# The last layer norm of a two-layer hybrid decoder: which tiles' statistics ScalarE forms, how epsilon is added, and how VectorE's work is ordered at the end

## The chip, the core and the metric

The kernel runs on one core of a Trainium2 chip. A core has five engines that run their own instruction streams in order and wait for each other on semaphores: TensorE (PE in the profile, its weight loads PEld), VectorE (DVE), ScalarE (ACT), GpSimd (POOL) and SyncE (SP, which here only issues transfers). SBUF is the on-chip memory of 128 partitions, PSUM the banks into which TensorE accumulates. The metric is the device time of one execution, in microseconds.

## The reference

Two post-norm layers over 1024 positions of width 1024. Layer 0 mixes tokens with a gated DeltaNet, layer 1 with an S5 state-space model; each has a memory attention beside its mixer and a squared-ReLU MLP behind it. What the change touches is the second norm of each layer:

```python
def layer_norm(x, g, b):
    xf = x.astype(jnp.float32)
    mu = jnp.mean(xf, axis=-1, keepdims=True)
    var = jnp.mean(jnp.square(xf - mu), axis=-1, keepdims=True)
    return ((xf - mu) * lax.rsqrt(var + LN_EPS) * g.astype(jnp.float32) + b.astype(jnp.float32)).astype(x.dtype)

for i in range(DEPTH):
    ...
    x = layer_norm(DN_ALPHA * x + h, ln1_g[i], ln1_b[i])
    f = jnp.square(jax.nn.relu(x @ mlp_w1[i])) @ mlp_w2[i]
    x = layer_norm(DN_ALPHA * x + f, ln2_g[i], ln2_b[i])
```

## The kernel before

Every product is formed from a high and a low part of each operand, as three matmuls of 128x512 into one PSUM bank (lines 397 to 399). The 1024 positions are eight tiles of 128 rows, tile 0 to tile 7.

The second half of the MLP (`mlp_second`) runs most of its products in a scheme with fewer multiplications and ends in `mlp_last`. There, for each tile and each half c of its 512 columns, TensorE runs a group of twelve matmuls into one of three PSUM banks in turn, VectorE adds the bank to the tile's row sum `y` (line 938), and after the second half `done` calls `layer_norm` for the tile. The text below writes 6a and 6b for the halves of tile 6.

`layer_norm` has two ways to its statistics. Without `junk`, VectorE runs one BN_STATS for each half (line 509), BN_AGGR (510) for mean and variance, and forms 1024 times (variance plus epsilon) (511). With `junk`, ScalarE sums each half (502), VectorE makes the negative mean (503), ScalarE sums the squares about it (505), and VectorE adds the two sums and epsilon (506). ScalarE must write its elementwise results somewhere; `junk` is a PSUM bank that nobody reads. GpSimd raises the result to the power -0.5 (512). VectorE then does two passes over the tile, called the centre (522: subtract the mean, times gamma) and the scale (523: times the power, plus beta). In the very last tile of the last layer the centre is line 514, and the scale runs in two halves (517), each stored at once (518). The factor 1024 leaves the power smaller by 32, so gamma is multiplied by 32 on ScalarE after it is loaded (2346 for the second norm, 2307 for the first).

In layer 0 the normalised tile goes through TensorE transposes (530) into the operands of layer 1, ScalarE and VectorE splitting them into high and low parts (534, 535). In layer 1 it is stored.

The order of instructions on every engine is not that of the code. `settle` takes all instructions of the program, their dependencies and a price for each, gives every instruction a due time from TensorE's sequence, and simulates the engines: on each, the open instruction that is due first goes next. The resulting order is fixed with dependencies. In that simulation an instruction may start when its predecessors' full length and a lag are over; a matmul behind a matmul needs only its busy time.

Constants lie at the start of SBUF in one pool, each in slots of 32 bytes; the pools of working tiles follow. In the built program before, the working tiles begin at byte 18,432 of a partition, and every one of the 3,288 tiles of 1 KB and more starts on a multiple of 512 bytes.

Of the kernel before, what the change touches and what calls it, by code (L numbers as in the profile page):

```python
# [10 lines left out]
F32 = mybir.dt.float32  # L11
F32R = mybir.dt.float32r
AF = mybir.ActivationFunctionType
ALU = mybir.AluOpType
AX = mybir.AxisListType

P = 128
# [16 lines left out]
class Trunk:  # L34
    def __init__(self, ctx, tc, a):
        self.tc = tc
        self.nc = nc = tc.nc
        self.a = a
        self.uid = 0
        self.turn = 0  # L40
        self.proj = 0
        self.soon = set()
        self.home, self.fixed = {}, set()
        self.cp = ctx.enter_context(tc.tile_pool(name="cp", bufs=1))
        self.sp = ctx.enter_context(tc.tile_pool(name="sp", bufs=1))
        self.ps = ctx.enter_context(tc.tile_pool(name="ps", bufs=1, space=bass.MemoryType.PSUM))
        self.dp = ctx.enter_context(tc.tile_pool(name="dp", bufs=1, space=bass.MemoryType.DRAM))
        self.ident = self.const("ident", [P, P])
        make_identity(nc, self.ident)
        self.const("pad", [P, 112])  # L50
        self.eps_ln = self.const("eps_ln", [P, 1])
        nc.gpsimd.memset(self.eps_ln, 1024 * 1e-5)
        self.mhalf = self.const("mhalf", [P, 4])
        nc.gpsimd.memset(self.mhalf, -0.5)
        self.half = self.const("half", [P, 4])
        nc.gpsimd.memset(self.half, 0.5)
# [5 lines left out]
    def settle(self, first, last, reach=0.0, ahead=15.0, passes=1, margin=0.0, late=0.0, hold=1e3):  # L62
# [118 lines left out]
        for _ in range(passes):  # L181
# [36 lines left out]
            while len(order) < n:  # L218
                first_ = None
                drift = free[E.PE] - due[turns[head]] if head < len(turns) else 0.0  # L220
                for e in names:
                    pick = None
                    for x in open_[e]:
                        if e == E.PE and x != turns[head] and due[x] > due[turns[head]] + reach - 1e-6:
                            continue
                        s = room(x) if fresh[x] else 0.0
                        if s is None:
                            continue
                        if e == E.SP:
                            s += 1  # L230
                        r = max(ready[x], s, free[e], due[x] - ahead if e != E.PE else 0.0)
                        if cost[x][2] > 1.5:
                            r = max(r, due[x] + drift - hold)
                        if e == E.PE and kind == "fr" and ins[x].ins[0].dtype == F32:
                            r += 0.15
                        other = 1.28 if sets[x] not in (None, table) else 0.0
                        k = (0, due[x] + other, r, x) if r <= free[e] + 0.1 else (1, r + other, due[x], x)
                        if pick is None or k < pick[0]:
                            pick = k, r, x
                    if pick and (first_ is None or pick[1:] < first_[1:]):  # L240
                        first_ = pick
                assert first_, f"no order: {len(order)} of {n}"
                r, x = first_[1:]
                e = ins[x].engine
                busy, length, moves = cost[x]
                if sets[x] not in (None, table):
                    table, busy, length = sets[x], busy + 1.28, length + 1.28
                if moves:
                    served = max(served, r + length - moves) + moves
                    length = served - r + late  # L250
                if port[x]:
                    r = max(r, locked)
                    locked = r + busy
                if e == E.PE:
                    lost += r - free[e]
                    kind = (kind + "fr"[ins[x].ins[0].dtype == F32R])[-2:]
                    gone.add(x)
                    while head < len(turns) and turns[head] in gone:
                        head += 1
                open_[e].remove(x)  # L260
                free[e] = r + busy
                order.append(x)
                for nm in fresh[x]:
                    t = self.home[nm][:2]
                    slots[t].remove(min(slots[t]))
                    turn[t].remove(nm)
                for y in after[x] + then[x]:
                    same = e == E.PE and ins[y].engine == e
                    ready[y] = max(ready[y], r + (0.0 if x not in deps[y] else busy if same else length + lag + (margin if ins[y].engine == E.PE else 0.0)))
                    wait[y] -= 1  # L270
                    if not wait[y]:
                        open_[ins[y].engine].append(y)
                for nm in uses(ins[x]):
                    if nm in users:
                        over[nm] = max(over[nm], r + length + (3 if ins[x].opcode == 'DMACopy' and e == E.Pool and self.home[nm][1] == 'gb' else 0.0))
                        todo[nm] -= 1
                        if not todo[nm] and nm not in behind and self.home[nm][:2] in slots:
                            slots[self.home[nm][:2]].append(over[nm] + lag)
# [214 lines left out]
    def layer_norm(self, y, gb, junk=None, last=None):  # L493

        nc = self.nc
        st = self.tile("st", [P, 2, 6], F32, "bn")
        halves = y if isinstance(y, list) else [y[:, c * HALF:(c + 1) * HALF] for c in range(2)]
        mv = self.tile("st", [P, 4], F32, "mv")
        if junk is not None:
            s = st.rearrange("p a b -> p (a b)")  # L500
            for c in range(2):
                nc.scalar.activation(junk, halves[c], AF.Copy, accum_out=s[:, c:c + 1])
            nc.vector.tensor_scalar(mv[:, 0:1], s[:, 0:1], s[:, 1:2], -1.0 / 1024, op0=ALU.add, op1=ALU.mult)
            for c in range(2):
                nc.scalar.activation(junk, halves[c], AF.Square, bias=mv[:, 0:1], accum_out=s[:, 4 + c:5 + c])
            nc.vector.scalar_tensor_tensor(mv[:, 2:3], s[:, 4:5], s[:, 5:6], self.eps_ln, op0=ALU.add, op1=ALU.add)
        else:
            for c in range(2):
                nc.vector.bn_stats(st[:, c, :], halves[c])
            nc.vector.bn_aggr(mv[:, 0:2], st)  # L510
            nc.vector.tensor_scalar(mv[:, 2:3], mv[:, 1:2], 1024.0, 1024 * 1e-5, op0=ALU.mult, op1=ALU.add)  # L511
        nc.gpsimd.tensor_tensor(mv[:, 3:4], mv[:, 2:3], self.mhalf[:, 0:1], op=ALU.pow)  # L512
        if last is not None:
            nc.vector.scalar_tensor_tensor(y, y, mv[:, 0:1], gb[0], op0=ALU.subtract, op1=ALU.mult)
            for c in range(2):
                c = slice(c * HALF, (c + 1) * HALF)
                nc.vector.scalar_tensor_tensor(y[:, c], y[:, c], mv[:, 3:4], gb[1][:, c], op0=ALU.mult, op1=ALU.add)
                nc.sync.dma_start(last[:, c], y[:, c])
            return
        parts = [(y, slice(0, 1024))] if not isinstance(y, list) else [(y[c], slice(c * HALF, (c + 1) * HALF)) for c in range(2)]  # L520
        for o, c in parts:
            nc.vector.scalar_tensor_tensor(o, o, mv[:, 0:1], gb[0][:, c], op0=ALU.subtract if junk is None else ALU.add, op1=ALU.mult)
            nc.vector.scalar_tensor_tensor(o, o, mv[:, 3:4], gb[1][:, c], op0=ALU.mult, op1=ALU.add)
# [1816 lines left out]
    def mlp_block(self, i, B, ahead, xd, side, out, more):  # L2340
        new = []

        def done(y, tau):
            if tau == 0:
                self.gb2 = self.load_gb(self.a["ln2_g"][i:i + 1], self.a["ln2_b"][i:i + 1])
                self.nc.scalar.activation(self.gb2[0], self.gb2[0], AF.Copy, scale=32.0)
                if more:
                    new.extend(self.new_xT())
            self.layer_norm(y[tau], self.gb2, self.psum("mm", "jk") if tau in ((), (5, 6))[i] else None, last=out[tau] if tau == 7 and not more else None)
            if tau < 7 or more:  # L2350
                self.nc.sync.dma_start(out[tau], y[tau])
            if more and tau == 7:
                self.last_x(y, new, more(new))
            elif more and tau < 6:
                self.transpose_x(y[tau], tau, new)
# [91 lines left out]
```

## Time and profile before

| | us |
|---|---|
| runs, median of 3 | 2513.36 |
| lowest and highest run | 2511.43, 2513.53 |
| the profiled execution | 2512.02 |
| its span in the profile | 2510.3 |
| TensorE busy | 2471.1 (98%) |
| VectorE busy | 1969.6 (78%) |
| ScalarE busy | 1283.0 (51%) |
| GpSimd busy | 435.9 (17%) |

The span is what the trace covers; the profiled execution's own time is 1.7 us longer. In the trace's timelines a row has the start, the duration, the engine, the line, the operation, the tiles written and read, and in brackets how long the engine idled before it and what ended that. A line is that of the kernel before.

### The profile page before, as it was taken

What the parts mean: (1) busy time and instruction counts of PE and PEld (TensorE: products, weight loads), DVE (VectorE), ACT (ScalarE), POOL (GpSimd) and SP (SyncE); (2) the same over time, 40 slices, a digit from 0 to 9 for tenths busy, and PEclk for the clock granted to TensorE, in tenths of its full rate; (3) what the DMA queues carried; (4) which work ended last, traced back from release to release, by engine and by line L of the source; (5) the groups of instructions that cost most, each with busy time, mean ns of one, the idle gap of its engine ahead of it and who ended that gap; (6) DMA issues with size and microseconds to landing.
All of it is one profiled execution on the core that took longest, in us unless ns stands there. A gap on an engine that the chain in (4) does not pass through costs nothing.

```text
span 2510.3 us, 36952 instructions
## 1 busy us (share of the span) xinstructions
PE 2471.1 (98%) x12181; PEld 2063.9 (82%) x12181; DVE 1969.6 (78%) x3676; ACT 1283.0 (51%) x2730; POOL 435.9 (17%) x673
## 2 busy tenths in 40 slices
PE   8999999999999999999999999999999999999998
PEld 6888887887887887888888888888887888888886
DVE  7786888777779798879988957786687666578788
ACT  6665555554556576554444244564365555544441
POOL 1232332414002023212210123112011000000000
PEclk9999999999999999999999999999999999999999
DMA  6464585767854567487454489669736434574532
GB/s 211 119 163 125 138 257 135 237 189 226 270 166 157 192 218 236 154 297 240 148 161 134 157 245 301 214 216 331 259 131 206 155 143 164 216 255 133 168 105 97
DMA packets 320769, 481.17 MB, mean 192 GB/s; under 512 B 110225, under 2 KB 141153, under 8 KB 320577
## 3 DMA queue, kind: packets, MB, share of 16 engines
q1 hardware_dynamic: 293056, 423.76, 51.9%
q0 software_dynamic: 25216, 50.86, 6.9%
q10 hardware_dynamic: 2304, 4.20, 0.4%
q8 instruction: 96, 1.57, 0.3%
q14 instruction: 97, 0.79, 0.1%
HBM read 321.91 MB, written 156.73 MB: 191 GB/s over the span
## 4 chain that ended last, share of the span: by engine, by line
PE 87%; DVE 5%; ACT 3%; DMA 2%; issue 2%; POOL 1%; SPq 0%; DVEq 0%; POOLq 0%; ACTq 0%
PE q L398 7%; PE q L397 7%; PE q L399 7%; PE tm L397 4%; PE tm L399 4%; PE tm L398 4%; PE pA L399 3%; PE pA L397 3%; PE pA L398 3%; PE wi L397 3%; PE wi L399 3%; PE wi L398 3%; PE pC L399 2%; PE pC L397 2%; PE pC L398 2%; PE pB L397 2%
## 5 line engine op out<-in xcount | busy, mean ns | idle before, releaser
L397 PE MATMUL q<-wkh,hkh 128*128 128x512 f32 x784 | 306.2, 391 | 0.7 <-ACT G L1886 0.7
L398 PE MATMUL q<-wkl,hkh 128*128 128x512 f32 x784 | 305.9, 390 | 0.5 <-DVE wkl L901 0.5
L399 PE MATMUL q<-wkh,hkl 128*128 128x512 f32 x784 | 305.4, 390 | 0.0
L900 ACT CAST wkh<-wr 128x512 fp32r<-128x512 f32 x168 | 104.9, 624 | 237.5 <-PE q L398 186.2
L512 POOL TENSOR_TENSOR mv<-mv,mhalf 128x1 f32<-128x1 f32 x32 | 26.7, 833 | 858.9 <-DVE mv L511 634.6
L397 PEld LDWEIGHTS q<-wkh,hkh 128*128 128x128 f32 x784 | 147.2, 188 | 32.2 <-ACT G L1886 1.6
L398 PEld LDWEIGHTS q<-wkl,hkh 128*128 128x128 f32 x784 | 147.3, 188 | 31.0 <-DVE wkl L901 1.1
L399 PEld LDWEIGHTS q<-wkh,hkl 128*128 128x128 f32 x784 | 147.2, 188 | 30.5
L901 DVE TENSOR_TENSOR wkl<-wr,wkh 128x512 fp32r<-128x512 f32 x168 | 115.5, 688 | 65.8 <-issue 55.6
L397 PE MATMUL wi<-xTh,wih 128*128 128x512 f32 x384 | 159.9, 416 | 0.2 <-ACT qT L1098 0.2
L398 PE MATMUL wi<-xTl,wih 128*128 128x512 f32 x384 | 152.6, 397 | 0.0
L399 PE MATMUL wi<-xTh,wil 128*128 128x512 f32 x384 | 152.4, 397 | 0.0
L901 DVE TENSOR_TENSOR hkl<-hr,hkh 128x512 fp32r<-128x512 f32 x196 | 133.9, 683 | 0.2 <-ACT hkh L900 0.2
L900 ACT CAST hkh<-hr 128x512 fp32r<-128x512 f32 x196 | 120.8, 616 | 1.3 <-DMA hr<-hd 1.2
L397 PE MATMUL tm<-so 128*128 128x512 f32 x280 | 109.8, 397 | 0.0
L1621 ACT CAST so<-or 128x1024 fp32r<-128x1024 f32 x70 | 72.0, 1049 | 59.5 <-DMA or<-wod 42.0
L1622 DVE TENSOR_TENSOR so<-or,so 128x1024 fp32r<-128x1024 f32 x70 | 84.5, 1220 | 16.1 <-ACT so L1621 16.0
L398 PE MATMUL tm<-so 128*128 128x512 f32 x224 | 88.2, 394 | 0.0
L399 PE MATMUL tm<-so 128*128 128x512 f32 x224 | 87.4, 391 | 0.0
L399 PEld LDWEIGHTS wi<-xTh,wil 128*128 128x128 f32 x384 | 72.7, 189 | 14.8
L397 PEld LDWEIGHTS wi<-xTh,wih 128*128 128x128 f32 x384 | 73.2, 191 | 12.5 <-ACT qT L1098 0.6
L398 PEld LDWEIGHTS wi<-xTl,wih 128*128 128x128 f32 x384 | 73.2, 191 | 11.6 <-issue 0.3
(588 smaller groups left out, 7381.8 us busy)
## 6 DMA issues: line engine op xcount, KB each, us to landing
hr<-hd SPq DMA_DIRECT2D x212, 256.0 KB, 2.8
wr<-in_w_dram SPq DMA_DIRECT2D x56, 512.0 KB, 5.0
hd<-u SPq DMA_DIRECT2D x92, 256.0 KB, 2.0
w1r<-in_w_dram SPq DMA_DIRECT2D x32, 512.0 KB, 3.5
hd<-hid SPq DMA_DIRECT2D x60, 256.0 KB, 2.3
hd<-p SPq DMA_DIRECT2D x60, 256.0 KB, 2.2
w1r<-in_w_dram SPq DMA_DIRECT2D x56, 256.0 KB, 3.6
wir<-in_w_in_dram SPq DMA_DIRECT2D x24, 512.0 KB, 3.9
```

The source lines that it names most:

```text
L397: mm(ps, a[0], b[0], start=start, stop=False, skip_group_check=onto)
L398: mm(ps, a[0], b[1], start=False, stop=False, skip_group_check=onto)
L399: mm(ps, a[1], b[0], start=False, stop=stop, skip_group_check=onto)
L512: nc.gpsimd.tensor_tensor(mv[:, 3:4], mv[:, 2:3], self.mhalf[:, 0:1], op=ALU.pow)
L900: nc.scalar.copy(hi, s)
L901: nc.vector.tensor_tensor(lo, s, f32(hi), op=ALU.subtract)
L1621: nc.scalar.copy(hi, r)
L1622: V.tensor_tensor(lo, r, f32(hi), op=ALU.subtract)
```

## The change

A constant of two columns, (0, epsilon), is added. Without `junk`, BN_AGGR now writes to two spare columns, and one addition of that constant yields mean and variance plus epsilon side by side; the centre reads the mean from there, so it needs the addition. With `junk`, the second norm (whose `y` is one tile, not a list of two) takes two operations for what was one: the scaled sum of squares, then epsilon. The first norm keeps its one operation. The second norm's power is then the true one, and ScalarE no longer multiplies its gamma by 32. In layer 1 ScalarE forms the statistics of tiles 3, 4 and 5 in place of 5 and 6. In `settle`, within the last 60 us of the simulated TensorE time, an instruction may follow its predecessor on the same engine after the busy time and 0.06 us.

```diff
         nc.gpsimd.memset(self.eps_ln, 1024 * 1e-5)
+        self.eps2 = self.const("eps2", [P, 2])
+        nc.gpsimd.memset(self.eps2[:, 0:1], 0.0)
+        nc.gpsimd.memset(self.eps2[:, 1:2], 1e-5)
         self.mhalf = self.const("mhalf", [P, 4])
...
                 for y in after[x] + then[x]:
-                    same = e == E.PE and ins[y].engine == e
-                    ready[y] = max(ready[y], r + (0.0 if x not in deps[y] else busy if same else length + lag + (margin if ins[y].engine == E.PE else 0.0)))
+                    same = ins[y].engine == e and (e == E.PE or not moves and spot[x] > now - 60.0)
+                    ready[y] = max(ready[y], r + (0.0 if x not in deps[y] else busy + (0.0 if e == E.PE else 0.06) if same else length + lag + (margin if ins[y].engine == E.PE else 0.0)))
...
-        mv = self.tile("st", [P, 4], F32, "mv")
+        mv = self.tile("st", [P, 6], F32, "mv")
...
-            nc.vector.scalar_tensor_tensor(mv[:, 2:3], s[:, 4:5], s[:, 5:6], self.eps_ln, op0=ALU.add, op1=ALU.add)
+            if isinstance(y, list):
+                nc.vector.scalar_tensor_tensor(mv[:, 1:2], s[:, 4:5], s[:, 5:6], self.eps_ln, op0=ALU.add, op1=ALU.add)
+            else:
+                nc.vector.tensor_scalar(mv[:, 4:5], s[:, 4:5], s[:, 5:6], 1.0 / 1024, op0=ALU.add, op1=ALU.mult)
+                nc.vector.tensor_tensor(mv[:, 1:2], mv[:, 4:5], self.eps2[:, 1:2], op=ALU.add)
         else:
             for c in range(2):
                 nc.vector.bn_stats(st[:, c, :], halves[c])
-            nc.vector.bn_aggr(mv[:, 0:2], st)
-            nc.vector.tensor_scalar(mv[:, 2:3], mv[:, 1:2], 1024.0, 1024 * 1e-5, op0=ALU.mult, op1=ALU.add)
-        nc.gpsimd.tensor_tensor(mv[:, 3:4], mv[:, 2:3], self.mhalf[:, 0:1], op=ALU.pow)
+            nc.vector.bn_aggr(mv[:, 4:6], st)
+            nc.vector.tensor_tensor(mv[:, 0:2], mv[:, 4:6], self.eps2, op=ALU.add)
+        nc.gpsimd.tensor_tensor(mv[:, 3:4], mv[:, 1:2], self.mhalf[:, 0:1], op=ALU.pow)
...
-                self.nc.scalar.activation(self.gb2[0], self.gb2[0], AF.Copy, scale=32.0)
...
-            self.layer_norm(y[tau], self.gb2, self.psum("mm", "jk") if tau in ((), (5, 6))[i] else None, last=out[tau] if tau == 7 and not more else None)
+            self.layer_norm(y[tau], self.gb2, self.psum("mm", "jk") if tau in ((), (3, 4, 5))[i] else None, last=out[tau] if tau == 7 and not more else None)
```

The new constant takes one 32-byte slot, and the working tiles of the built program begin at byte 18,464 in place of 18,432: of the tiles of 1 KB and more, all but one lie 32 bytes further on.

The line numbers of the changed kernel are 7 higher in the second half of `layer_norm` and behind it: the centre is 529, the scale 530, BN_STATS 516, BN_AGGR 517, the new addition 518 (513 with `junk`), the addition from PSUM 945. On VectorE, the end of the program stood so before (`mv_24285` belongs to tile 6, `mv_24325` to tile 7):

```order
L506 SCALAR_TENSOR_TENSOR mv_24285<-bn_24284,eps_ln 128x1
L522 SCALAR_TENSOR_TENSOR y_21712<-y_21712,mv_24285,gb_24047 128x1024
L938 TENSOR_TENSOR y_21712<-tm_24310,y_21712 128x512
L523 SCALAR_TENSOR_TENSOR y_21712<-y_21712,mv_24285,gb_24049 128x1024
L509 BN_STATS bn_24324<-y_21712 128x6
L510 BN_AGGR mv_24325<-bn_24324 128x2
L514 SCALAR_TENSOR_TENSOR y_21712<-y_21712,mv_24325,gb_24047 128x1024
L511 TENSOR_SCALAR mv_24325<-mv_24325 128x1
L517 SCALAR_TENSOR_TENSOR y_21712<-y_21712,mv_24325,gb_24049 128x512 x2
```

and now so (`mv_24253` is tile 5, `mv_24294` tile 6, `mv_24332` tile 7):

```order
L518 TENSOR_TENSOR mv_24294<-mv_24294,eps_74 128x2
L529 SCALAR_TENSOR_TENSOR y_21714<-y_21714,mv_24294,gb_24049 128x1024
L945 TENSOR_TENSOR y_21714<-tm_24303,y_21714 128x512
L516 BN_STATS bn_24331<-y_21714 128x6
L530 SCALAR_TENSOR_TENSOR y_21714<-y_21714,mv_24253,gb_24051 128x1024
L530 SCALAR_TENSOR_TENSOR y_21714<-y_21714,mv_24294,gb_24051 128x1024
L945 TENSOR_TENSOR y_21714<-tm_24317,y_21714 128x512
L516 BN_STATS bn_24331<-y_21714 128x6
L517 BN_AGGR mv_24332<-bn_24331 128x2
L518 TENSOR_TENSOR mv_24332<-mv_24332,eps_74 128x2
L521 SCALAR_TENSOR_TENSOR y_21714<-y_21714,mv_24332,gb_24049 128x1024
L524 SCALAR_TENSOR_TENSOR y_21714<-y_21714,mv_24332,gb_24051 128x512 x2
```

The epsilon step has moved ahead of the centre of tile 7, and the scales of tiles 5 and 6 stand together ahead of the addition of 7b, with its statistics directly behind it. On VectorE in layer 0, the norm of tile 0 was, from its BN_AGGR to its scale:

```order
L510 BN_AGGR mv_14463<-bn_14462 128x2
L938 TENSOR_TENSOR y_11658<-tm_14486,y_11658 128x512
L522 SCALAR_TENSOR_TENSOR y_11658<-y_11658,mv_14463,gb_14453 128x1024
L511 TENSOR_SCALAR mv_14463<-mv_14463 128x1
L509 BN_STATS bn_14514<-y_11658 128x6
L921 TENSOR_TENSOR hk_14374<-hr_14366,hk_14373 128x512
L523 SCALAR_TENSOR_TENSOR y_11658<-y_11658,mv_14463,gb_14455 128x1024
```

and is now:

```order
L517 BN_AGGR mv_14465<-bn_14464 128x2
L945 TENSOR_TENSOR y_11661<-tm_14488,y_11661 128x512
L518 TENSOR_TENSOR mv_14465<-mv_14465,eps_74 128x2
L516 BN_STATS bn_14516<-y_11661 128x6
L529 SCALAR_TENSOR_TENSOR y_11661<-y_11661,mv_14465,gb_14456 128x1024
L928 TENSOR_TENSOR hk_14377<-hr_14369,hk_14376 128x512
L530 SCALAR_TENSOR_TENSOR y_11661<-y_11661,mv_14465,gb_14458 128x1024
```

The epsilon step and the next tile's BN_STATS have moved ahead of the centre; the scale has the same operations ahead of it. On TensorE only the transposes of four tiles in that norm move, back by one matmul for three of them and by four for the last. No other matmul of the program changes place; ScalarE loses the two multiplications of gamma and gains the third tile's sums; SyncE's queue changes in two neighbouring pairs of loads.

## The prediction

> **What bounds the kernel now.** I read the page first, then TensorE's own waits, then the end of the chain of waits.
>
> ```profile
> span 2510.3 us, 36952 instructions
> PE 2471.1 (98%) x12181; PEld 2063.9 (82%) x12181; DVE 1969.6 (78%) x3676; ACT 1283.0 (51%) x2730; POOL 435.9 (17%) x673
> PE 87%; DVE 5%; ACT 3%; DMA 2%; issue 2%; POOL 1%; SPq 0%; DVEq 0%; POOLq 0%; ACTq 0%
> PE ba L1011 <- ACT xTh L993: 7.9, 2, 7.2
> PE po L1432 <- ACT on L1460: 4.3, 5, 2.4
> ```
>
> TensorE is busy for 2471.1 of 2510.3 us. Of the 39 us left over, 7.9 us are one wait at the start and 4.3 us the next largest; both lie far from the norms that are edited. The rest worth having is behind the last matmul. The PE timeline has, as the last matmul of each half tile's group of twelve:
>
> ```profile
> 2494.54 0.39 PE L399 MATMUL tm<-w2h,hk 128*128 128x512 f32 x1
> 2497.26 0.39 PE L399 MATMUL tm<-w2h,hk 128*128 128x512 f32 x1
> 2499.98 0.39 PE L399 MATMUL tm<-w2h,hk 128*128 128x512 f32 x1
> ```
>
> TensorE ends at 2499.98 + 0.39 = 2500.37, so 9.9 us of the span are a tail. Half tiles come 2.72 us apart: 6b (second half of tile 6) at 2494.9, 7a at 2497.65, 7b at 2500.4. VectorE's timeline shows what is done with them:
>
> ```profile
> 2489.52 0.69 DVE L938 TENSOR_TENSOR y<-tm,y 128x512 f32<-128x512 f32 x1 [0.24 <-PE tm L399]
> 2491.32 0.21 DVE L503 TENSOR_SCALAR mv<-bn 128x1 f32<-128x1 f32 x1
> 2492.24 0.69 DVE L938 TENSOR_TENSOR y<-tm,y 128x512 f32<-128x512 f32 x1 [0.71 <-PE tm L399]
> 2493.26 0.22 DVE L506 SCALAR_TENSOR_TENSOR mv<-bn,eps_ln 128x1 f32<-128x1 f32 x1 [0.33 <-ACT jk L505]
> 2493.40 1.28 DVE L522 SCALAR_TENSOR_TENSOR y<-y,mv,gb 128x1024 f32<-128x1024 f32 x1
> ...
> 2499.94 1.28 DVE L522 SCALAR_TENSOR_TENSOR y<-y,mv,gb 128x1024 f32<-128x1024 f32 x1
> 2501.14 0.69 DVE L938 TENSOR_TENSOR y<-tm,y 128x512 f32<-128x512 f32 x1
> 2501.74 1.28 DVE L523 SCALAR_TENSOR_TENSOR y<-y,mv,gb 128x1024 f32<-128x1024 f32 x1
> 2502.93 0.69 DVE L509 BATCH_NORM_STATS2 bn<-y 128x6 f32<-128x512 f32 x1
> 2503.65 0.21 DVE L510 BATCH_NORM_AGGREGATE mv<-bn 128x2 f32<-128x12 f32 x1
> 2503.90 1.28 DVE L514 SCALAR_TENSOR_TENSOR y<-y,mv,gb 128x1024 f32<-128x1024 f32 x1
> 2505.10 0.15 DVE L511 TENSOR_SCALAR mv<-mv 128x1 f32<-128x1 f32 x1
> 2505.97 1.41 DVE L517 SCALAR_TENSOR_TENSOR y<-y,mv,gb 128x512 f32<-128x512 f32 x2 [0.73 <-POOL mv L512]
> ```
>
> Half 7b could be added at 2500.4 and is added at 2501.14, behind tile 6's centre (L522); its statistics wait again behind tile 6's scale (L523). At the very end VectorE idles 0.73 us for GpSimd's power, which was asked for only after the last centre (L514).
>
> **The change, part by part.** Two prices come from these rows. Independent operations follow each other 0.08 to 0.1 us before the record of the first ends (L522 at 2499.94, the next at 2501.14: 1.20 for a record of 1.28). An operation that needs its predecessor's result starts 0.03 to 0.04 us after its end (L509 ends 2503.62, L510 starts 2503.65; L510 ends 2503.86, L514 starts 2503.90). GpSimd's rows hold the third:
>
> ```profile
> 2485.31 0.55 POOL L512 TENSOR_TENSOR mv<-mv,mhalf 128x1 f32<-128x1 f32 x1 [4.64 <-DVE mv L511]
> 2493.63 1.46 POOL L512 TENSOR_TENSOR mv<-mv,mhalf 128x1 f32<-128x1 f32 x1 [3.65 <-DVE mv L506]
> 2500.17 1.46 POOL L512 TENSOR_TENSOR mv<-mv,mhalf 128x1 f32<-128x1 f32 x1 [5.08 <-DVE mv L506]
> 2505.39 0.55 POOL L512 TENSOR_TENSOR mv<-mv,mhalf 128x1 f32<-128x1 f32 x1 [3.76 <-DVE mv L511]
> ```
>
> A power takes 0.55 us while VectorE is idle or adds from PSUM, but 1.46 us when a centre from SBUF started just before it: at 2500.17 the centre ends at 2501.22 and the power at 2501.63, 0.41 us later. That matters, because the change puts the power exactly there: mean and epsilon now come before the centre, so the power starts under it.
>
> *Epsilon ahead of the centre, last tile.* Before, from L510 to L517: 2505.97 - 2503.65 = 2.32. After: L510 0.21 + 0.03; the new addition, which no row shows, lies between L511 (0.15, no tensor scalar) and L506 (0.22, three operands) and I take 0.20, + 0.03; centre 1.28; power 0.41 behind it, + 0.03: 2.19. The gain is 0.13, not the whole 0.73, since the power is held under the centre. If it were not held, L517 would follow the centre's end by 0.03: 1.78, a gain of 0.54. Those are the ends.
>
> *ScalarE's statistics for tiles 3 to 5 in place of 5 and 6.* Tile 5 keeps its ScalarE chain; its rows:
>
> ```profile
> 2490.31 0.60 ACT L502 ACTIVATE jk<-y 128x512 f32<-128x512 f32 x1 [1.77 <-DVE y L938]
> 2491.57 0.69 ACT L505 ACTIVATE jk<-y,mv 128x512 f32<-128x512 f32 x1 [0.53 <-DVE mv L503]
> 2493.05 0.18 ACT L505 ACTIVATION_READ_ACCUMULATOR jk<-y,mv 128x1 f32 x1
> ```
>
> From the second sum to the last accumulator are 2.9 us, more than a half tile's 2.72. For tiles 3 and 4 this lies before 2489.5, beside VectorE work that keeps up with TensorE (it idles 0.24 at 2489.52), so nothing on the end; without that cover a tile would cost its 2.9 less the 1.4 of two L509. The waiting instruction is the variance on VectorE; the centre and the next half's addition are queued behind it, and TensorE, with three banks for these sums, would wait only if an addition came more than two groups late. Tile 6 goes back to VectorE: two L509 (0.69 each) and L510 more, no ScalarE turn.
>
> *VectorE's order behind 6a.* I follow the new row order from 2492.24, where both orders wait for TensorE. 6a added 2492.24; its L509 2492.96; tile 5's variance 2493.57; centre 2493.69; epsilon 2494.89; 6b added 2495.01; L509 2495.73; L510 2496.45; epsilon 2496.69; tile 6's centre 2496.92; 7a added 2498.12; L509 2498.84; the scales of 5 and 6 at 2499.45 and 2500.65; 7b added 2501.85; L509 2502.57; L510 2503.29; then 2.19 to the first scale of tile 7: 2505.48. Before it was 2505.97. So 7b is added 0.71 later than before, but the scale that stood between it and its statistics is gone: **0.49 us less**, of which 0.36 is order and 0.13 the power. With a power not held: 0.90.
>
> Behind it nothing changes: the two halves (1.41), the store, the end of the span. SyncE's queue holds only stores there: tile 5's now comes after 2500.7, with tile 6's behind it, and both scales are done 3.5 us ahead of the first scale of tile 7.
>
> *The layer-0 norm* makes the same move eight times, with TensorE behind it:
>
> ```profile
> 1395.13 1.28 DVE L523 SCALAR_TENSOR_TENSOR y<-y,mv,gb 128x1024 f32<-128x1024 f32 x1
> 1396.85 1.03 PE L530 MATMUL xt<-ident,y 128*128 128x128 f32 x8
> ```
>
> Tile 0's scale ends at 1396.41, its transposes start 0.44 later; the new order puts the same operations ahead of the scale, and the transposes of four tiles one or four matmuls (0.23 us each) later. The addition costs VectorE some 0.06 per tile over L511. Hidden: 0. If the cover is gone, eight tiles lose 0.06 for the addition and up to 0.13 where a power and a centre start together: 1.5 us.
>
> *The scaling of gamma by 32* leaves ScalarE (two of 1.06 us, in an engine at 51%): 0. *Two more memsets* on GpSimd at the start, and the work pool 32 bytes further on:
>
> ```profile
> 0.97 0.10 POOL L54 MEMSET mhalf<- 128x4 f32 x1
> 7.18 0.63 PE L1011 MATMUL ba<-xTh,wbah 128*32 128x512 f32 x1 [7.18 <-ACT xTh L993]
> L1100 DVE SCALAR_TENSOR_TENSOR kT<-cv,scr,kT 128x512 f32<-128x512 f32 x48 | 35.8, 745 | 5.3 <-ACT kT L1098 4.9
> L523 DVE SCALAR_TENSOR_TENSOR y<-y,mv,gb 128x512 f32<-128x512 f32 x32 | 22.8, 744 | 0.0
> ```
>
> Memsets of that size (the row is 0.10) end 6 us before TensorE's first matmul waits for a load: 0. The shifted addresses touch every instruction. For VectorE the trace has the comparison: L1100 reads `cv` 0, 4 and 8 bytes past a boundary and takes 745 ns, L523 reads aligned tiles in 744. No row shows TensorE or a large transfer at an address off a 64-byte multiple. I take 0 from the nearest row, VectorE's, and keep the loss for the rivals.
>
> Sum: the profiled execution is 2512.02 us, its span 2510.3 and 1.7 around it; it becomes 2511.5. The runs' median is 1.34 above that execution, so **2512.9**.
>
> **The rivals.**
>
> *Shifted transfers slow the kernel (the other side).* Every load into SBUF and every store from it now starts 32 bytes off. Place: the stretches in which the transfers have no time to spare.
>
> ```profile
> q1 hardware_dynamic: 293056, 423.76, 51.9%
> 1500.00:1600.00 100.00, 100.00 (x581) 87.95 (x580) 68.37 (x128) 48.52 (x76) 31.89 (x45) 1.00 1.00 300
> 1700.00:1800.00 100.00, 100.00 (x443) 82.84 (x442) 63.47 (x72) 39.70 (x48) 10.74 (x8) 1.00 0.91 311
> ```
>
> In the windows the DMA share (last but one) is 1.00 and 0.91. If packets take longer by a part x, 100x us come out in the first, and 91x - 9 in the second where that is above 0. It decides (5 us) from x = 0.055; at 1/16 it gives 2512.9 + 6.3 = 2519, at 1/8 2512.9 + 12.5 + 2.4 = 2528. Against it: TensorE is 100% busy in both windows, so the loads run ahead of it, and over the span q1 has half its time free. TensorE reading shifted operands more slowly belongs here too: 3% of a matmul of 0.23 us, 7 ns, over some 10,000 of the page's 12181 would be 70 us; nothing in the trace speaks for it.
>
> [...] No run here shows a shifted row.
>
> *The gain is given back in layer 0*: transposes stand in TensorE's order, and a late scale stops everything behind them. Price 0 to 1.5: 2512.9 to 2514.4. Against it the 0.44 us of slack and the later transposes.
>
> *The change does not do what it says*: power held longer than 0.41, or 7b's lateness outweighs; 2513.4.
>
> *Faster by more than 5 us*: half of the 9.9 us tail would have to go, while the work behind 7b alone (L938, L509, L510, centre, two halves) is over 4 us before the store; or the shifted addresses help.
>
> **How the numbers follow.** A measurement of this kernel can tell about 0.2%, 5.0 us, from no change. Forecast 0.58 and the two small rivals 0.17 together all lie within it: same 0.75. Shifted addresses 0.22: slower. Faster 0.03. The likeliest's own range is 2511.5 to 2514.4 (both ends of the tail, the layer-0 loss, and the spread of the three runs, 2511.43 to 2513.53). For 8 in 10 I reach up to the rival's 1/16 and a little beyond, 2520, and down to 2510.8, leaving about 0.12 above and 0.05 below.
>
> **What would show it.** Right: in the tail the first scale of tile 7 some 5.1 us after the last matmul's end (5.6 before), its power 1.4 to 1.5 us long under the centre, no scale between 7b's addition and its statistics, TensorE's last matmul at 2500 as before. The power's row at 0.55 would mean the larger gain. Wrong: TensorE's end moved by more than 1 us. Then the DMA share of 1500 to 1600 and the transfers' times to landing, TensorE's pitch of 0.23 us, and the gaps ahead of the transposes at 1396 to 1440 say which rival it was.

## The result, and the profile after

| | before | after |
|---|---|---|
| runs, median (us) | 2513.36 (9 runs) | 2520.23 (9 runs) |
| lowest and highest (us) | 2510.85, 2516.41 | 2516.78, 2522.43 |
| profiled execution, its span (us) | 2512.02, 2510.3 | 2521.06, 2519.3 |
| last matmul's end to the end of the span (us) | 9.93 | 9.39 |
| last matmul's end to the first scale of tile 7 (us) | 5.60 | 5.06 |

The ratio of the medians is 1.0028, with a 95% interval of 1.0018 to 1.0039: the changed kernel is slower by 6.9 us. The tail became 0.54 us shorter, as forecast (0.49). The loss is in the middle of the program. The page of the changed kernel begins so (span, busy times, then the shares of the chain that ended last):

```profile
span 2519.3 us, 36970 instructions
PE 2475.1 (98%) x12181; PEld 2065.5 (82%) x12181; DVE 1972.1 (78%) x3677; ACT 1284.3 (51%) x2736; POOL 439.2 (17%) x675
PE 83%; DMA 6%; DVE 4%; ACT 2%; issue 2%; POOL 1%; SPq 1%; POOLq 0%; DVEq 0%; ACTq 0%
```

The share of DMA on the chain was 2% and is 6%: at some place the end now hangs on transfers. TensorE's waits (line waited for, us in total, times, longest) name the place. Two rows are there that the kernel before does not have at all:

```profile
PE py L1978 <- DMA H<-h1d: 2.8, 3, 1.3
PE p L1952 <- DMA s5t<-ud: 2.5, 2, 1.4
```

Both belong to the S5 stage of layer 1, and the window on it (TensorE's, its weight loads', VectorE's, ScalarE's and GpSimd's busy time with counts, then granted clock, DMA share, GB/s) is to be read beside the row that the prediction quotes:

```profile
1500.00:1600.00 100.00, 95.10 (x540) 82.76 (x539) 66.65 (x124) 46.40 (x72) 32.59 (x46) 1.00 1.02 289
1700.00:1800.00 100.00, 99.58 (x445) 82.09 (x444) 62.66 (x83) 40.71 (x57) 13.35 (x9) 1.00 0.90 310
```

The transfers were at a share of 1.00 before and are so after, but they move 289 GB/s for 300, and TensorE, never idle in this window before, runs 540 matmuls for 581. The second window is nearly what it was. Matching each matmul of 512 columns of one trace with the same matmul of the other, both counted from the start of their span, I find TensorE 2.2 us late at 1473 and 8.7 us late at 1602: 6.5 us arise in these 130 us, and later matmuls keep that distance but for 0.8 more at 1752 to 1786.

The 2.2 us ahead of that stage are 1.7 won at the start and several small losses behind it. The two largest, 1.2 at 416 to 449 and 1.8 at 960 to 996, go with the granted clock and not with the loads. In the same columns, before:

```profile
416.00:449.00 33.00, 29.40 (x154) 24.56 (x153) 29.23 (x61) 17.56 (x61) 18.61 (x30) 0.95 0.49 121
960.00:1000.00 40.00, 38.29 (x170) 31.38 (x169) 33.97 (x87) 25.55 (x45) 15.71 (x28) 1.00 0.67 221
```

and after:

```profile
416.00:449.00 33.00, 29.41 (x148) 24.75 (x147) 28.74 (x57) 16.93 (x60) 18.69 (x30) 0.90 0.52 136
960.00:1000.00 40.00, 38.07 (x161) 31.05 (x160) 33.90 (x87) 24.43 (x44) 15.71 (x28) 0.96 0.70 230
```

The clock records of the traces show it: near 440 us the clock is at half for 3.4 us before and for 6.8 us after, and near 993 us for 3.4 us in the trace after alone. The traces of kernels without the loss have such stretches too: the one shifted by 256 bytes (below) loses 1.2 us at 416 to 449, and the edits without the shift lose 1.9 us at 960 to 996.

The transfers of that stage, from issue to landing (line by line: tiles, queue, count, size, median us), before:

```profile
tab<-tabd POOLq DMA_DIRECT2D x32, 256.0 KB, 5.4
G<-g1d POOLq DMA_DIRECT2D x16, 256.0 KB, 10.8
s5t<-ud SPq DMA_DIRECT2D x8, 512.0 KB, 10.3
H<-h1d POOLq DMA_DIRECT2D x16, 256.0 KB, 11.5
```

and after:

```profile
tab<-tabd POOLq DMA_DIRECT2D x32, 256.0 KB, 8.0
G<-g1d POOLq DMA_DIRECT2D x16, 256.0 KB, 11.9
s5t<-ud SPq DMA_DIRECT2D x8, 512.0 KB, 11.3
H<-h1d POOLq DMA_DIRECT2D x16, 256.0 KB, 13.5
```

All of them became later by 1.0 to 2.6 us, though the change edits nothing near them. The engines' own durations stayed (a matmul of 128x512 391 ns in both profiles, the subtraction of a split 683 and 687).

The tail after, by VectorE's and GpSimd's timelines and the last matmul:

```profile
2509.52 0.39 PE L402 MATMUL tm<-w2h,hk 128*128 128x512 f32 x1
2511.36 0.69 DVE L945 TENSOR_TENSOR y<-tm,y 128x512 f32<-128x512 f32 x1
2512.08 0.69 DVE L516 BATCH_NORM_STATS2 bn<-y 128x6 f32<-128x512 f32 x1
2512.80 0.21 DVE L517 BATCH_NORM_AGGREGATE mv<-bn 128x2 f32<-128x12 f32 x1
2513.05 0.16 DVE L518 TENSOR_TENSOR mv<-mv,eps 128x2 f32<-128x2 f32 x1
2513.25 1.29 DVE L521 SCALAR_TENSOR_TENSOR y<-y,mv,gb 128x1024 f32<-128x1024 f32 x1
2513.38 1.56 POOL L519 TENSOR_TENSOR mv<-mv,mhalf 128x1 f32<-128x1 f32 x1 [5.24 <-DVE mv L518]
2514.97 1.41 DVE L524 SCALAR_TENSOR_TENSOR y<-y,mv,gb 128x512 f32<-128x512 f32 x2 [0.44 <-POOL mv L519]
```

TensorE ends at 2509.52 + 0.39 = 2509.91. No scale stands any more between the addition of 7b (L945) and its statistics (L516). The power starts under the centre, takes 1.56 us and ends at 2514.94, 0.40 behind the centre's end, and the first scale waits 0.44 us for it.

### The profile page after: what moved, and what is told of

The parts are those of the page before. It is cut to its first block, busy times and chain, and to the rows that moved or that the text cites. A ratio compares the mean times of both kernels' runs of the same rounds, so it can differ in the third digit from the quotient of the medians.

```text
span 2519.3 us, 36970 instructions
## 1 busy us (share of the span) xinstructions
PE 2475.1 (98%) x12181; PEld 2065.5 (82%) x12181; DVE 1972.1 (78%) x3677; ACT 1284.3 (51%) x2736; POOL 439.2 (17%) x675
## 4 chain that ended last, share of the span: by engine, by line
PE 83%; DMA 6%; DVE 4%; ACT 2%; issue 2%; POOL 1%; SPq 1%; POOLq 0%; DVEq 0%; ACTq 0%
PE q L401 7%; PE q L400 7%; PE q L402 7%; PE tm L400 4%; PE tm L402 4%; PE tm L401 4%; PE pA L402 4%; PE pA L400 3%; PE pA L401 3%; PE wi L400 3%; PE wi L402 3%; PE wi L401 3%; PE pC L402 2%; PE pC L401 2%; PE pC L400 2%
```

## The experiments

The changed kernel does two separate things: it edits the norms and the planner, and its new constant puts the working tiles 32 bytes further on. Theory: the 32 bytes alone make the loss, because transfers whose SBUF side begins off some boundary take longer. Rival: the edits make it. In all comparisons below the runs of the kernel before were taken on the same chip in turn with the kernel's own.

**The edits without the shift** (of the changed kernel; the pad is an unused constant, 8 columns are 32 bytes):

```diff
-        self.const("pad", [P, 112])
+        self.const("pad", [P, 104])
```

> The whole change, with the unused constant ahead of it cut from 112 to 104 columns, so that the working tiles begin at byte 18,432 again. Theory (the shifted addresses cost the time, the norm's edits gain): the tail of 9.9 us becomes 9.4, the S5 stage has no waits of TensorE on transfers, and the run is 2512.8, 0.4 to 0.6 us below the kernel before. Rival (the new order of VectorE, GpSimd and the loads costs the time): 2518 to 2521, as with the change.

Measured: 2512.83 us for 2513.34, ratio 1.0000 (0.9991 to 1.0009). Its first scale of tile 7 is 5.04 us behind the last matmul's end, and 9.35 us of the span are tail. The loss is gone and the tail's gain is kept. One clause of the expectation missed: in the profiled execution, which took 2516.94 us, TensorE waited 1.7 us for H in the S5 stage.

**The shift without the edits** (of the kernel before, `pad` 112 columns):

```diff
-        self.const("pad", [P, 112])
+        self.const("pad", [P, 120])
```

> The kernel before with the unused constant 8 columns wider: every working tile 32 bytes further on, nothing else. Theory: 2519 to 2522, with TensorE waiting for transfers between 1500 and 1600 us and a DMA share of 1.0 there at less than 300 GB/s. Rival (order): 2513.4, no such waits.

Measured: 2520.5 us, ratio 1.0032 (1.0019 to 1.0045). The same order of instructions on every engine as before, all tiles 32 bytes further, and the whole loss is there. The window and the wait are those of the changed kernel:

```profile
1500.00:1600.00 100.00, 97.08 (x549) 84.50 (x550) 68.47 (x127) 45.85 (x71) 31.93 (x45) 1.00 1.02 287
PE py L1971 <- DMA H<-h1d: 3.1, 3, 1.2
```

**Other distances**, in the same way: 64 bytes (pad 128), 128 (144), 256 (176) and 512 (240).

> The kernel before with every working tile 64 bytes further on. If only addresses off a multiple of 64 cost, 2513.4, as before. If a block of 256 bytes or more must be met, 2519 to 2522, as with 32. Rival (order): 2513.4.

> The kernel before with every working tile 512 bytes further on: other addresses, the same alignment to 512. Theory (alignment): 2513.4, within 1.5 us. A rival (any other placement of the tiles costs, aligned or not, or the kernel before is a lucky one): 2517 or more.

> The kernel before with its working tiles 256 bytes further than before (a multiple of 256, no more of 512). Theory (what counts is whether a row begins on a 512-byte boundary): 2515 to 2518 us, like the shift of 64. Rival (a boundary of 256 is enough): 2513 us, like the shift of 512.

> The kernel before with its working tiles 128 bytes further. Theory (512 counts, and the cost falls with the alignment that is left): 2515 to 2517 us. If a boundary of 64 or 128 were enough it would be 2513; but the shift of 64 already cost 4 us, so for 128 to be free the limit would be 128.

| shift (bytes) | median (us) | ratio to before, interval | 512 B packets at exactly 27 ns | GB/s, 1500 to 1600 | TensorE's loss, 1473 to 1602 (us) |
|---|---|---|---|---|---|
| 0 | 2513.34, with 128 and 256 2513.35 | | 16024 of 16576 | 300 | |
| 32 | 2520.50 | 1.0032 (1.0019 to 1.0045) | 9844 | 287 | 5.1 |
| 64 | 2517.35 | 1.0016 (1.0008 to 1.0025) | 10679 | 284 | 7.0 |
| 128 | 2517.12 | 1.0012 (1.0003 to 1.0021) | 11100 | 292 | 4.6 |
| 256 | 2512.62 | 0.9998 (0.9990 to 1.0007) | 15927 | 299 | 0.1 |
| 512 | 2512.30 | 0.9998 (0.9988 to 1.0007) | 15987 | 296 | 2.2 |

The packets (the fourth column, my count over one trace each, SyncE's queue) separate the shifts into two groups, and so do the times: of the distances tried, those that leave the tiles on a multiple of 256 bytes cost nothing. Of the two expectations for 256 the rival's came true, not that of a 512-byte boundary. The result for 64 lies between its two expectations and fits neither; that for 128 is 0.1 us above its own. The intervals of 32, 64 and 128 overlap, so whether 32 costs more than the others is open.

The last column compares one trace each with the trace before, by the same matmuls. Of the 7.0 us at 64, some 1.7 are an estimate for 3.4 us at half clock near 1541. The edits without the shift lost 2.2 us there, so one execution of a kernel on multiples of 256 can be late as well; the medians carry the size of the loss, the column its place. The profile shows 256 like 0, TensorE without a gap:

```profile
1500.00:1600.00 100.00, 100.00 (x580) 87.94 (x580) 68.42 (x128) 48.31 (x76) 31.85 (x45) 1.00 0.98 299
```

**Transfers by themselves.** All computation is replaced by phases of 48 transfers of 512 KB at six offsets of the SBUF side:

```diff
+        OFFS = [0, 8, 16, 32, 64, 0]
+        for off in OFFS:
+            fence()
+            load(nc.sync, off, 1024)
...
+                    nc.sync.dma_start(tl[k % n][:, b:b + 512].rearrange("p (j e) -> p j e", e=128), v[:, h])
```

> The whole computation is left out: only transfers of 512 KB tiles run, 48 to a phase, with the SBUF side 0, 32, 64, 128, 256 and again 0 bytes behind a multiple of 512, the phases kept apart by short VectorE operations. Phases: loads on SP's queue, stores on SP's queue, loads on GpSimd's queue, loads and stores mixed, and loads cut into runs of 512 bytes. Theory (a transfer itself takes longer when its SBUF rows begin off a 512-byte boundary): a phase of saturated transfers lasts 3 to 7% longer at +32 than at 0, as the window 1500-1600 suggests (287 GB/s for 300), less at +64, and the last phase of 0 repeats the first. Rival (the shift costs only where engines use SBUF at the same time, or by which bank two tiles fall in): all six phases of a kind agree within 1%. Which kind shows it tells where to look: if loads show it and stores do not, writing into SBUF is the slow side.

Windows of one phase each (VectorE and GpSimd busy, clock, DMA share, GB/s). Loads of 4 KB rows at +0 and +32, stores at +32 and +128, loads and stores mixed at +32:

```profile
30.00:60.00 30.00, 0.00 (x0) 0.00 (x0) 1.00 1.03 420
90.00:130.00 40.00, 0.64 (x6) 0.00 (x0) 1.00 1.03 409
455.00:495.00 40.00, 0.85 (x8) 0.00 (x0) 1.00 1.03 420
580.00:620.00 40.00, 1.06 (x10) 0.00 (x0) 1.00 1.02 405
1190.00:1220.00 30.00, 0.00 (x0) 0.00 (x0) 1.00 1.03 420
```

and loads in runs of 512 bytes at +0, +32, +256 and again +0:

```profile
1490.00:1540.00 50.00, 1.06 (x10) 0.00 (x0) 1.00 1.13 339
1570.00:1620.00 50.00, 0.64 (x6) 0.00 (x0) 1.00 1.17 290
1825.00:1875.00 50.00, 1.38 (x13) 0.00 (x0) 1.00 1.15 346
1895.00:1945.00 50.00, 0.85 (x8) 0.00 (x0) 1.00 1.14 343
```

With the engines all but idle, a saturated queue of loads loses 2.6% (409 for 420) when its 4 KB rows are 32 bytes off, and 15% (290 for 343) when it writes runs of 512 bytes; at 256 it loses nothing (420 and 346). GpSimd's queue loses as much with 4 KB rows (410 at +32 for 420 at +256). So the slowness of loads is the transfer's own. Stores at +32 lose nothing (420) and at +128 3.6% (405 for 420); half loads and half stores lose nothing at any offset (419 to 420). The expected 3 to 7% for a phase was thus too much for long rows and too little for short ones, and the expected smaller loss at +64 did not come: +64 and +128 lose as much as +32 (410, 410 for long rows, 290, 290 for short ones). The S5 stage is neither of these cases: most of its bytes are loads, some are stores. Its 4% lie between the two losses of pure loads, but no run derives them.

**Which tiles.** Pads between the groups of working tiles put some of them 32 bytes off and leave the others on a multiple of 256 (of the kernel before; the second kernel is the complement). Each pad is an unused tile ahead of the first of its group:

```diff
-        self.const("pad", [P, 112])
+        self.const("pad", [P, 48])
...
+    PADS = {"h1": 8, "raw": 56, "xT": 8, "gb": 56, "h2": 8, "h3": 56}
...
+        if tag in self.pads:
+            k = self.pads.pop(tag)
+            self.sp.tile([P, k], F32, tag="pad" + tag, name="pad" + tag, bufs=1)
```

> The kernel before, with pads between the working tiles so that only those of the tags h1, xT and h2 begin 32 bytes behind a multiple of 256, and all others on one. These three hold what the S5 stage loads in runs of 512 bytes: G, H, tab, and s5t. Theory (the shift costs where a saturated queue writes short runs into shifted tiles that TensorE waits for, so mainly the S5 stage): 2518 to 2520 us, most of the 7 that the shift of all tiles cost, and a window 1500-1600 under 293 GB/s with H and s5t on TensorE's list of waits. Rival (the cost is spread over all transfers, by bytes): about half or less, 2515 to 2517.

> The complement: tags h1, xT and h2 on multiples of 256, all other working tiles (the weights' raw and split tiles, gb, h5, h3, h4, the small ones) 32 bytes behind one. Theory: 2513 to 2515 us, the window 1500-1600 near 299 GB/s as with a shift of 256 or 512. Rival (cost spread by bytes, or tiles that only engines use): 2516 to 2518.

Measured: 2537.02 us (ratio 1.0097, 1.0084 to 1.0111) and 2530.15 (1.0070, 1.0057 to 1.0083), for 2512.85: 24.2 and 17.3 us, both far above what any theory expected. Together they cost six times what they cost when all tiles move at once, so a part of it cannot be the transfers. It is TensorE's. The groups of matmuls (line, tiles, count, busy us, mean ns, idle before) of the first of the two:

```profile
L402 PE MATMUL q<-wkh,hkh 128*128 128x512 f32 x784 | 306.2, 391 | 0.4 <-ACT G L1891 0.4
...
L402 PE MATMUL wg<-xTh,wgh 128*128 128x512 f32 x128 | 50.8, 397 | 0.0
```

and before:

```profile
L397 PE MATMUL q<-wkh,hkh 128*128 128x512 f32 x784 | 306.2, 391 | 0.7 <-ACT G L1886 0.7
...
L397 PE MATMUL wg<-xTh,wgh 128*128 128x512 f32 x128 | 50.1, 392 | 0.0
```

Some products are slower and some are not. I took, for 9,277 matmuls of 512 columns with a successor, the SBUF address of the streamed operand, the address of the successor's weights (loaded meanwhile) and the time between the two starts:

```
                                         kernel 1             kernel 2
addresses equal modulo 256     5,481 matmuls, 227 ns   5,481 matmuls, 227 ns   (median from start to start)
addresses not equal            3,796 matmuls, 234 ns   3,796 matmuls, 234 ns
the latter before the pads                    227 ns                  227 ns
sum of their differences                     17.1 us                 17.8 us
```

This is a cost of the experiment's own, since it moves operands against each other; a shift of all tiles does not. Taken off, the transfers' part is 24.2 - 17.1 = 7.1 us with the tiles of tags h1, xT and h2 shifted, and 17.3 - 17.8 = -0.5 with all others. As estimates (sums of one trace against medians, good to about 1 us) they say that the tiles of these three tags carry the whole loss. Among them are all into which S5 loads G, H, tab and s5t, but also other loads, so it is not shown that those four alone make it. The windows agree (first kernel, then second):

```profile
1500.00:1600.00 100.00, 98.02 (x542) 83.56 (x541) 67.07 (x125) 46.51 (x73) 34.76 (x50) 1.00 1.03 291
PE py L1976 <- DMA H<-h1d: 1.4, 3, 0.9
```

```profile
1500.00:1600.00 100.00, 100.00 (x558) 85.92 (x557) 70.23 (x131) 48.45 (x75) 33.73 (x48) 1.00 0.99 297
```

The second has no wait of TensorE for an S5 transfer. One clause of the expectation is not borne out by the trace: it called all these loads runs of 512 bytes, but on GpSimd's queue, which carries G, H and tab, the records are packets of 4,096 bytes, and the run length within one cannot be seen. In 1475 to 1615 their mean is 226 ns before, 247 with all tiles at +32, 215 at +256.

**The tail.** Three variants of the change without the shift. First, the last centre in two halves:

```diff
-            nc.vector.scalar_tensor_tensor(y, y, mv[:, 0:1], gb[0], op0=ALU.subtract, op1=ALU.mult)
+            for c in range(2):
+                c = slice(c * HALF, (c + 1) * HALF)
+                nc.vector.scalar_tensor_tensor(y[:, c], y[:, c], mv[:, 0:1], gb[0][:, c], op0=ALU.subtract, op1=ALU.mult)
```

> The change with its working tiles where the kernel before has them (the pad is 8 columns shorter), and the last tile's centring in two halves of 512 columns. Theory (GpSimd's power is held while VectorE's 1024-column centring runs and ends 0.41 us behind it): the power gets in between the two halves or ends earlier against the last of them, the first scale waits for it no more than 0.1 us, and it stands 4.7 to 4.8 us behind the last matmul's end (5.04 without the split): about 0.3 us less in the tail, 2512.5 us, too little for the median alone to show. Rival (the power takes its 1.5 us wherever the centring stands, from its own latency): the wait of the first scale stays 0.4 us and a further VectorE instruction adds 0.1.

Measured: 2511.76 us for 2513.35, ratio 0.9994 (0.9985 to 1.0003). From its timeline:

```profile
2499.55 0.39 PE L402 MATMUL tm<-w2h,hk 128*128 128x512 f32 x1
2503.26 1.42 DVE L523 SCALAR_TENSOR_TENSOR y<-y,mv,gb 128x512 f32<-128x512 f32 x2
2503.39 1.03 POOL L519 TENSOR_TENSOR mv<-mv,mhalf 128x1 f32<-128x1 f32 x1 [5.25 <-DVE mv L518]
2504.59 1.41 DVE L526 SCALAR_TENSOR_TENSOR y<-y,mv,gb 128x512 f32<-128x512 f32 x2
```

The power takes 1.03 us in place of 1.56 and ends inside the second half (2504.42), the first scale waits for nothing, and it starts 4.65 us behind the last matmul's end. The first half takes 0.75 us, so the power ends 0.41 us behind it, as it ended 0.40 behind the whole centre. So the power's length is set by the centre's operation under which it starts, not by the power's own latency. The tail is 8.96 us, nearly 1 us shorter than before; the medians cannot show as little.

Second, with ScalarE on tiles 5 and 6 as before and the split centre:

```diff
-... if tau in ((), (3, 4, 5))[i] else None ...
+... if tau in ((), (5, 6))[i] else None ...
```

> The change with its working tiles where the kernel before has them, ScalarE forming the statistics of tiles 5 and 6 as before instead of 3 to 5, and the last centring in two halves. Theory (what the split saves adds to what the choice of tiles gives in the tail): the first scale 4.0 to 4.5 us behind the last matmul's end (4.7 or so with tiles 3 to 5 and the split), 2511 to 2512.5 us. Rival (without tiles 3 to 5 on ScalarE VectorE is late at the end, as the change supposes): 4.7 or later, 2512 to 2513.

Measured: 2512.57 us for 2512.85, ratio 1.0000 (0.9991 to 1.0009). The first scale is 5.26 us behind the last matmul's end, 0.61 later than with tiles 3 to 5: the theory fell, the rival holds.

Third, the edits of epsilon and gamma alone, the planner's rule as before too:

```diff
-                    same = ins[y].engine == e and (e == E.PE or not moves and spot[x] > now - 60.0)
+                    same = e == E.PE and ins[y].engine == e
```

> The change with its working tiles where the kernel before has them, with ScalarE's tiles 5 and 6 and the planner's rule as before: of the change only the addition of epsilon ahead of the centring and the scaling of gamma are left. The prediction's split of the tail (0.13 from epsilon, 0.36 from the order) asks for the first scale 5.4 to 5.5 us behind the last matmul's end, against 5.60 before and 5.05 with the whole change. Rival (the order does all of it): 5.6. Rival (epsilon does all of it): 5.05.

Measured: one execution of 2512.91 us, first scale 6.01 us behind the last matmul's end (2500.85). All three expectations missed, since each took the order of before for given. The rows:

```profile
2497.55 1.28 DVE L530 SCALAR_TENSOR_TENSOR y<-y,mv,gb 128x1024 f32<-128x1024 f32 x1 [0.73 <-POOL mv L519]
2498.75 0.21 DVE L506 TENSOR_SCALAR mv<-bn 128x1 f32<-128x1 f32 x1
...
2504.70 0.20 DVE L517 BATCH_NORM_AGGREGATE mv<-bn 128x2 f32<-128x12 f32 x1
...
2506.86 1.41 DVE L524 SCALAR_TENSOR_TENSOR y<-y,mv,gb 128x512 f32<-128x512 f32 x2 [0.45 <-POOL mv L519]
```

From L517 to the first scale are 2.16 us for 2.32: that gain is there. But VectorE waits 0.73 us for tile 5's power ahead of tile 6's mean (L506), which comes 0.41 us later against TensorE than before; the addition of 7b behind it is 0.40 late, the second step of tile 6's epsilon stands ahead of 7b's statistics, and tile 7's L517 comes 3.85 us behind the last matmul for 3.28 before.

## Why the prediction was wrong

**The step that failed** is the term for the shifted addresses: "I take 0 from the nearest row, VectorE's, and keep the loss for the rivals." It measured 7.2 us (2520.50 for 2513.34, shift alone). The nearest row was one of another kind: an engine reading SBUF at 745 or 744 ns says nothing of a queue writing into it, which lost 2.6 to 15% of its rate. For the engines the step was right (391 ns a matmul in both).

**The rival that came true** is "Shifted transfers slow the kernel", at its lower price: 6.3 us at x = 1/16 in the window 1500 to 1600, for a loss of 6.9 with the tail's 0.5 won against it. The place was right, and so was the second window's small part: with the shift alone 5.1 of the 5.5 us by which its trace is longer arise in the stage. That the size came out is in part luck. No row stood behind x = 1/16, and no run shows it; the rate in that window fell by 3.7% (289 for 300), or 4.3% with the shift alone (287), so x was too large, and the stage is 130 us long where the price had 100. The small losses around 430 and 980 us are not part of this rival, since they go with the clock, nor is it shown that the 0.8 at 1752 to 1786 is (at +512 it was 1.1).

**The argument against it fell**: "TensorE is 100% busy in both windows, so the loads run ahead of it." A window without idle time says that the loads are not late, not by how much they are early. H and s5t took 10 to 12 us from issue to landing at a DMA share of 1.00, and with 1.0 to 2.6 us more TensorE waited. Even unshifted kernels can be late there: the edits alone waited 1.7 us for H in their profile, at +512 it was 1.5. Here a share of 1.00 under a full TensorE meant two limits that touch, and it should have raised the chance of this rival above 0.22.

**The rival's upper price**, x = 1/8, is shown by no run either. With no computation beside them, loads lost 2.6% of their rate with rows of 4 KB (409 GB/s for 420) and 15% with runs of 512 bytes (290 for 343), which is 2.7% and 18% more time; the S5 window lost 3.7%.

**TensorE reading shifted operands** was priced at "3% of a matmul of 0.23 us, 7 ns" with nothing in the trace for it. A common shift costs it nothing (227 ns from start to start with all tiles at +32). A shift of one operand by 32 bytes against the other costs 7 ns, as the pads between the tiles showed; that this is the figure of the prediction is luck.

**The tail's step was right**: first scale 5.06 us behind TensorE (forecast 5.11), L517 to L524 2.17 (2.19), the addition 0.16 (0.20), the power held 0.40 behind the centre's end (0.41), 0.54 us of the span (0.49). The split into 0.13 for epsilon and 0.36 for the order is no sum of independent parts, though: with the epsilon edit alone the first scale comes 0.41 us later than before, and the order makes 0.97 good (6.01 to 5.04). The planner lays out every instruction anew, so the row order of the very kernel must be followed, as the forecast did for the whole change.

**The other terms**: gamma's scaling, the memsets and the layer-0 norm at 0 stand; TensorE's distance between the two traces is the same at 1386 and 1448 to 0.1 us. The edits alone are at 2512.83, ratio 1.0000; the forecast of 2512.9, made for a shift that costs nothing, is met by them, though the runs alone could not tell it from no change.

## What to carry to other kernels

A constant of a few bytes ahead of the working tiles moves every tile behind it, so compare the addresses of two builds before comparing anything else, and keep tiles that a busy queue loads on multiples of 256 bytes (here 7 us of 2513 hung on it). Check as well that the two operands of a matmul lie alike modulo 256; 32 bytes between them cost 7 ns a matmul here. Where a window shows transfers at a share of 1.00 under a TensorE that never idles, ask for the time from landing to use before taking the loads as hidden. Where two traces drift apart, read the granted clock of the stretch before giving the drift to a cause.

## What the runs showed of the hardware

- Loads into SBUF lost rate 32 bytes behind a multiple of 512, also with the engines all but idle: 2.6% for rows of 4 KB (409 GB/s for 420) and 15% for runs of 512 bytes (290 for 343), as much at +64 and +128, and nothing at +256 (420 and 346). Stores from SBUF lost nothing at +32 (420) and 3.6% at +128 (405), and a half and half mix of both nothing (419 to 420). Why stores and the mix differ was not tried.
- TensorE's pitch (from start to start) is 227 ns when the streamed operand and the next weights begin at addresses equal modulo 256, and 234 ns when they begin 32 bytes apart (3,796 matmuls in each of two kernels). Other distances were not tried.
- GpSimd's power on one column took 0.55 us beside an idle VectorE, 1.46 or 1.56 under a centre of 1,024 columns and 1.03 under one in two halves of 512. In the tails of the kernels before, after and with the split centre it ended 0.40 to 0.41 us behind the centre's operation that was running when it started.
- The granted clock fell to half for 3.4 or 6.8 us at a time near 440 and 577 us in the traces before and after, and near 993 us in the one after. Where one trace had 3.4 us more of it than the other, TensorE lost 1.2 us (416 to 449) and 1.8 us (960 to 996).
